# Context sums inside the latent mixer, 96 gathered tokens in both expert layers, and routing in tiles of 128 tokens

## The chip, the core and the metric

The kernel runs on one NeuronCore of a Trainium2 chip. The metric is the device time of one execution in microseconds. Five queues of instructions matter here: PE (TensorE, matrix multiplies; the load of the stationary operand is shown apart as PEld), DVE (VectorE), ACT (ScalarE), POOL (GpSimd, which also issues the gathers of table rows) and SP (which issues the loads of weights). Each runs its instructions in the order in which they were written into it. Everything is in fp32. One matrix multiply of the program is two instructions on PE in the trace, so that counts of the trace are twice those of the program.

## The reference, cut to what matters

The program is a transformer of two layers (`first_block`) whose output is the latent sequence of a second model (`second_block`): 256 latent tokens and 256 context tokens of width 1024. What the change touches lies in the second model:

- a mixer with a recurrent state in layer 0 (`deltanet_mixer`), first over the context, then over the latent tokens, which starts from the state that the context left,
- an attention in layer 1, for which the context gives keys and values,
- after each of them a layer of experts (`peer`), for the context only in layer 0:

```python
qry = (xb @ w_query).reshape(P, PEER_HEADS, 2, PEER_HALF)
s = jnp.einsum('phcd,hckd->phck', qry, sub_keys)
top_s, top_i = lax.top_k(s, PEER_TOPK)          # 16 of 128 keys, two halves, 8 heads
...                                             # the best 16 of the 16 x 16 pairs of each head
act = jax.nn.gelu(jnp.einsum('pd,phkd->phk', xb, u_tab[idx]))
coef = gate * act
return jnp.einsum('phk,phkd->pd', coef, v_tab[idx])
```

So each token has 128 experts out of 16384, with one row of 1024 numbers (4 KB) in `u_tab` and one in `v_tab` for each. A gather of 128 rows is 512 KB.

## The kernel before, in words

**Stages.** In order of time: the context's mixer; the routing of the context's experts (`peer_prep`); the first model, with the context's expert gathers beside it; the latent mixer (`deltanet(E, x, ..., "dl")`); the latent expert layer 0 (`lat_peer(E, 0, ...)`) with the keys of the context for the attention (`ctx_keys`) inside it; the attention; the latent expert layer 1; a last norm.

**Experts of the context.** The dot products with `u_tab` (`gather_dot`) run for all 256 tokens beside the first model. Of the weighted sums over `v_tab`, those of tokens 0 to 127 run there too, on PE (`gather_sum_pe`): for four tokens at a time four gathers bring 128 rows each, eight matrix multiplies of 32 x 512 form the sums (two halves of 512 columns; the four tokens write to different 32 partitions of one PSUM bank), two ACT copies bring them out and one DMA stores four rows. The sums of tokens 128 to 255 run in the latent expert layer 0, on DVE (`bg` and `gather_sum`: 128 gathers, and for each one DVE instruction that adds 128 weighted rows).

**Experts of the latent tokens.** Each layer splits its 256 tokens. The first `NB` of them (64 in layer 0, 96 in layer 1) are gathered: 16 gathers of `u_tab` rows and 16 of `v_tab` rows for each 16 tokens, with one DVE instruction for each (`Few`). The other 192 or 160 tokens go through all 16384 experts densely (`Dense`): 128 tiles of 128 experts, of which each takes 8 multiplies with a tile of `u_tab` (`up`, PE lines `au<-hp,ut`), a gelu and a product with the token's gates in the matrix `G`, and later 8 multiplies with `v_tab` in two halves (`down`, `y<-G,vt`). The gates enter `G` by `spread`: for four tokens a time ACT and DVE make one-hot factors (`ohl`, `ohr`) and PE multiplies them (`gp<-ohr,ohl`). Every tile of `u_tab` or `v_tab` is a load of 512 KB. In time a layer is: routing multiplies (`acs<-hp,w`), the ups with the spreads among them, the first half of the downs, the second half.

**Routing** (`peer_route`). The query multiplies run over all 256 tokens at once (16 tiles of weights, 128 x 256 each); the sorting of the scores (DVE) for the first 128 tokens runs between them, that for the second 128 after them, while the ups go on (`weave`). When a tile of tokens is routed, PE transposes its indices and gates (L1843). The indices of the gathered tokens go through DRAM into another layout (`route`: `gtb`, `ixb`, `fix`).

**What sets the order.** A scheduler puts the instructions of each engine in order from the order in which the program writes them and from its own estimate of times. The side work is written by generators: `start` sets one and its rate, and `tick(E, us)`, called after each tile of the main work, writes `us * rate` steps of it. With `paced` set, such a step is put behind the instruction `E.pin`. In layer 0 the gathers start after the second tile is routed (a factor `z` that is made from the last index and is zero holds them), in layer 1 at up 24 (`FAT`). Gathered rows and weight tiles of a layer share one ring of buffers (`E.wp`, tag `w`, 10 of 512 KB; 8 in the latent mixer, for weights alone).

## Time and profile before

| what | value |
|---|---|
| median of 3 runs (lowest, highest) | 3986.34 us (3985.33, 3995.86) |
| the profiled execution | 3984.59 us, of which its span is 3982.8 us |
| granted clock of PE, mean over the span | 0.951 |
| PE busy | 3528.3 us (89%), 22501 instructions |
| PEld busy | 2828.7 us (71%) |
| DVE, POOL, ACT busy | 2318.4 us (58%), 1247.7 us (31%), 1129.6 us (28%) |
| moved by DMA | 1028.78 MB, mean 258 GB/s |

How to read it: the share of the span that an engine is busy is a mean over stages that differ. Matrix multiplies overlap, so that a group's busy time divided by its count is what one costs in a row, while the "mean ns" of a row is the length of one with its overlap. The granted clock is the share of full speed at which PE was let run. The column "DMA share" is the busy share of the 16 DMA engines; a share of 1 goes with 370 to 400 GB/s here.

The stages by their first and last instructions, for orientation: latent mixer 1668 to 2168 us, latent expert layer 0 2184 to 3099 us, attention until 3225 us, latent expert layer 1 3229 to 3972 us.

### The profile page before, as it was taken

How to read it: one execution, taken by the hardware profiler on the slowest of the kernel's cores; microseconds unless marked ns; L12 is line 12 of the kernel's file. 1: busy time of each engine (PE TensorE's matmuls, PEld its weight loads, DVE VectorE, ACT ScalarE, POOL GpSimd, SP SyncE). 2: the span in 40 equal slices, each digit the busy share in tenths (PEclk: the TensorE clock that was granted, in tenths of full speed). 3: DMA queues.
4: the chain of work that ended last, by engine and by line, in shares of the span. 5: the costliest groups of instructions: out<-in, count | busy, mean ns of one | idle time of the engine just before them, and what ended most of it. 6: DMA issues, size and time to landing. Idle time of an engine off the chain costs nothing. (4 is left out here: it accounts for less than half of the span.)

```text
span 3982.8 us, 60769 instructions
## 1 busy us (share of the span) xinstructions
PE 3528.3 (89%) x22501; PEld 2828.7 (71%) x22501; DVE 2318.4 (58%) x5519; ACT 1129.6 (28%) x3199; POOL 1247.7 (31%) x1169
## 2 busy tenths in 40 slices
PE   7787988979999889888888979988899999998998
PEld 6664564638746458466545979987899668998898
DVE  4774348758646578377732667974530438684442
ACT  4233212634315444242222124720000312470000
POOL 1110004553344553211000255544521104333331
PEclk9898998989999889999999999999999999999999
DMA  5444353899998899633633569999995435999996
GB/s 196 120 141 149 127 179 118 288 332 347 337 343 313 293 328 349 218 118 109 239 115 116 165 260 387 353 392 369 399 340 171 159 95 192 386 356 391 396 392 255
DMA packets 373527, 1028.78 MB, mean 258 GB/s; under 512 B 84240, under 2 KB 86608, under 8 KB 372464
## 3 DMA queue, kind: packets, MB, share of 16 engines
q1 hardware_dynamic: 227728, 557.36, 39.6%
q0 software_dynamic: 119808, 436.26, 29.5%
q10 hardware_dynamic: 25696, 31.28, 2.6%
q8 instruction: 178, 2.92, 0.3%
q14 instruction: 117, 0.96, 0.1%
HBM read 1008.88 MB, written 15.89 MB: 257 GB/s over the span
## 5 line engine op out<-in xcount | busy, mean ns | idle before, releaser
L392 PE MATMUL y<-G,vt 128*128 128x192 f32 (+1 forms) x4096 | 641.2, 316 | 58.4 <-DMA vt<-in_peer_v_dram 58.0
L392 PE MATMUL au<-hp,ut 128*128 128x192 f32 (+1 forms) x4096 | 651.6, 317 | 29.9 <-DMA ut<-in_peer_ut_dram 25.7
L392 PEld LDWEIGHTS y<-G,vt 128*128 128x128 f32 x4096 | 615.0, 191 | 82.8 <-DMA vt<-in_peer_v_dram 64.5
L392 PEld LDWEIGHTS au<-hp,ut 128*128 128x128 f32 x4096 | 624.5, 193 | 40.5 <-issue 29.0
L392 PE MATMUL acc<-hdn,w 128*128 128x256 f32 x1536 | 371.4, 395 | 41.6 <-DVE cvu L1253 16.1
L1697 POOL DMA_INDIRECT gu<-in_peer_u_dram,ixs x256 | 278.8, 1089 | 344.7 <-DVE gu L1699 242.7
L1699 DVE SCALAR_TENSOR_TENSOR gu<-gu,h 128x1024 f32<-128x1024 f32 x256 | 312.0, 1225 | 103.4 <-DMA gu<-in_peer_u_dram,ixs 101.4
L392 PEld LDWEIGHTS acc<-hdn,w 128*128 128x128 f32 x1536 | 292.2, 196 | 96.5 <-issue 23.1
L1718 DVE SCALAR_TENSOR_TENSOR fy<-gv,fc,fy 128x1024 f32<-128x1024 f32 x150 | 192.8, 1285 | 201.6 <-DMA gv<-in_peer_v_dram,fix 201.3
L1789 DVE SCALAR_TENSOR_TENSOR fg<-fg,fh 128x1024 f32<-128x1024 f32 x160 | 193.2, 1227 | 134.6 <-DMA fh<-hl_d 52.6
L1775 POOL DMA_INDIRECT fg<-in_peer_u_dram,fix x160 | 186.7, 1167 | 252.2 <-PE au L392 76.1
L1713 POOL DMA_INDIRECT gv<-in_peer_v_dram,fix x160 | 182.9, 1143 | 244.7 <-PE y L392 204.1
L1713 POOL DMA_INDIRECT gv<-in_peer_v_dram,ixz x128 | 160.1, 1250 | 139.5 <-DVE y L1718 78.8
L1718 DVE SCALAR_TENSOR_TENSOR y<-gv,col,y 128x1024 f32<-128x1024 f32 x127 | 162.8, 1282 | 50.1 <-DMA gv<-in_peer_v_dram,ixz 49.2
L1736 POOL DMA_INDIRECT gv<-in_peer_v_dram,ixT x128 | 140.9, 1101 | 143.2 <-DVE gu L1699 88.2
L392 PE MATMUL acs<-hff,w 128*128 128x256 f32 x704 | 168.7, 380 | 0.0
L392 PE MATMUL acs<-xs,sh 128*128 128x256 f32 x704 | 150.5, 310 | 1.3 <-POOL xs L530 0.8
L392 PEld LDWEIGHTS acs<-hff,w 128*128 128x128 f32 x704 | 126.5, 190 | 21.0 <-issue 7.5
L1456 POOL TENSOR_TENSOR ob<-ob,qs 128x256 f32<-128x256 f32 x32 | 25.0, 781 | 368.2 <-ACT qs L1454 269.0
L1253 DVE SCALAR_TENSOR_TENSOR cvu<-acc,vec,cvu 128x255 f32<-128x255 f32 (+1 forms) x256 | 121.7, 480 | 31.2 <-ACT cvu L1250 29.0
L1943 ACT ACTIVATE ys<-y,ada 128x192 f32<-128x192 f32 (+1 forms) x16 | 5.3, 409 | 455.3 <-PE y L392 455.3
L392 PE MATMUL acs<-hp,w 128*128 128x256 f32 x512 | 117.8, 386 | 8.4 <-DMA w<-in_peer_wq_dram 7.5
(603 smaller groups left out, 6150.4 us busy)
## 6 DMA issues: line engine op xcount, KB each, us to landing
ut<-in_peer_ut_dram SPq DMA_DIRECT2D x256, 512.0 KB
vt<-in_peer_v_dram SPq DMA_DIRECT2D x256, 512.0 KB
w<-in_ada_w_dram SPq DMA_DIRECT2D x96, 512.0 KB
w<-in_dn_w_in_dram SPq DMA_DIRECT2D x96, 512.0 KB
w<-in_w_up_dram SPq DMA_DIRECT2D x88, 512.0 KB
w<-in_peer_wq_dram SPq DMA_DIRECT2D x48, 512.0 KB
wd<-in_w_down_dram SPq DMA_DIRECT2D x44, 512.0 KB
w<-in_w_in_dram SPq DMA_DIRECT2D x40, 512.0 KB
```

The source lines that it names most:

```text
L392: return E.nc.tensor.matmul(out, lhsT=lhsT, rhs=rhs, start=start, stop=stop)
L1253: nc.vector.scalar_tensor_tensor(out=u[:, os], in0=p[:, is_], scalar=cw[tap][:, ct:ct + 1], in1=u[:, os], op0=ALU.mult, op1=ALU.add)
L1456: nc.gpsimd.tensor_tensor(out=ov, in0=ov, in1=qs, op=ALU.add)
L1697: nc.gpsimd.indirect_dma_start(out=g, out_offset=None, in_=E.a["peer_u"], in_offset=bass.IndirectOffsetOnAxis(ap=ix[:, s, k:k + 1], axis=0))
L1699: nc.vector.scalar_tensor_tensor(out=g, in0=g, scalar=1.0, in1=h, op0=ALU.mult, op1=ALU.mult, accum_out=c[:, k:k + 1])
L1713: nc.gpsimd.indirect_dma_start(out=g, out_offset=None, in_=E.a["peer_v"], in_offset=bass.IndirectOffsetOnAxis(ap=ix[:, k:k + 1], axis=0))
L1718: nc.vector.scalar_tensor_tensor(out=y, in0=g, scalar=c[:, k:k + 1], in1=y, op0=ALU.mult, op1=ALU.add)
L1736: nc.gpsimd.indirect_dma_start(out=g, out_offset=None, in_=E.a["peer_v"], in_offset=bass.IndirectOffsetOnAxis(ap=ix, axis=0))
L1775: self.E.nc.gpsimd.indirect_dma_start(out=g, out_offset=None, in_=self.E.a[tab], in_offset=bass.IndirectOffsetOnAxis(ap=self.ix[:, s, k:k ...
L1789: nc.vector.scalar_tensor_tensor(out=g, in0=g, scalar=1.0, in1=h, op0=ALU.mult, op1=ALU.mult, accum_out=self.c[:, s, k:k + 1])
L1943: nc.scalar.mul(s[:, k, nb:256], self.y[k][:, 0:T], g2[:, n * 4 + k:n * 4 + k + 1])
```

## The change

Five edits:

1. The sums of context tokens 128 to 255 leave layer 0 and its DVE code `bg`. They run beside the latent mixer, by `gather_sum_pe`, as 8 groups of 16 tokens. A step of them (one gather; after each fourth also the multiplies, the copies and the store) is written by the mixer's ticks at a rate of `LRATE` = 0.42 per microsecond of its estimated work. The gathered rows take buffers of the mixer's weight ring (`E.wp`), which has 7 instead of 8; the sums take PSUM banks of the tag `ps`, of which the mixer has 2. For this the second tile's indices are transposed as well (`ixT[1]`).
2. Layer 0 gathers 96 tokens instead of 64, as layer 1 does; its dense part has 160 instead of 192. The rate of the gather steps is 0.165 in both, and the second half of the downs is cut at tile 56 instead of 48 (`LAST`).
3. Routing of the latent layers runs one tile of 128 tokens at a time: the query multiplies are 128 x 128, and every tile of query weights is loaded and multiplied twice. In `peer_route` the code for `lin1` does this.
4. The gathers of a layer start as soon as the first tile is routed (`routed`), without the factor `z`. The transposes of the routed indices for both tiles are written 60 steps later (`LAG`), behind an up's last multiply.
5. In `spread` all four `ohl` get the gate on ACT (four instructions of 128 columns instead of two of 128 and one of 256), and DVE makes `ohr` in one instruction of 512 columns instead of one of 256 and two of 128.

```diff
@@ peer_route
+    for ts in ((0, 1),) if lin1 is None else ((0,), (1,)):
+        n = 128 * len(ts)
+        for cidx in range(4):
+            q = PI.tile([128, 4, n], F32, name="pq", bufs=2)
+            ...
+                lin1(ts[0], *z)
+            for j, tt in enumerate(ts):
...
+            if ts[0] == 0:
+                drain(top(0, range(cidx * 4, cidx * 4 + 4)))
@@ gather_sum_pe
-    p = bank(E, "gy", "gy")
+    tag = "gy" if "gy" in E.xps else "ps"
+    p = bank(E, tag, "gy")
-            g = R.tile([128, D], F32, name="gv", tag="g")
-            ix = ixT[:, s * 16 + t + j:s * 16 + t + j + 1]
+            g = (R or E.wp).tile([128, D], F32, name="gv", tag="g" if R else "w")
+            ix = ixT[s // 8][:, s % 8 * 16 + t + j:s % 8 * 16 + t + j + 1]
@@ Dense.prep
-            lin = lambda *z: lin_cols_split(E, PU, None, *z, tag="y", xf=self.x)
+            def lin(tt, ap, off, nt, fn):
+                for t in range(nt):
+                    p = bank(E, "y", "acs")[:, 0:128]
+                    ws = wtile(E, ap, off + t * D * 128, 2, 512)
+                    for k in range(8):
+                        mm(E, p, ws[k // 4][:, k % 4 * 128:k % 4 * 128 + 128], self.x[:, k, tt * 128:tt * 128 + 128],
+                           k == 0, k == 7)
+                    fn(t, p)
...
             def done(t, idx, gate, idf):
                 if t == 0:
                     self.few.route(idx, gate)
+                    routed()
+                found.append((idf[0], idf[1], gate))
+            yield from peer_route(E, P, P, WK, self.i, None, done, lin)
+            for _ in range(LAG):
+                yield
+            for t in range(2):
                 p = pst(E)
+                with tc.issue_after(self.pe):
+                    for j, src in enumerate(found[t]):
+                        nc.tensor.transpose(p[:, j * 128:j * 128 + 128], fl(src), E.ident)
@@ Dense.spread
-        a = 2
-        for j in range(a):
+        for j in range(4):
             nc.scalar.activation(L[:, j], L[:, j], AF.Relu, scale=col(3, j), bias=col(2, j))
-        nc.scalar.activation(L[:, a:4], L[:, a:4], AF.Relu, bias=1.0, scale=-1.0)
-        ...
-        for j in range(a, 4):
-            nc.vector.tensor_scalar(R[:, j], self.iota, col(0, j), col(2, j), op0=ALU.is_equal, op1=ALU.mult)
+        E.pin = nc.vector.tensor_tensor(out=R, in0=self.iota[:, None, :].to_broadcast([128, 4, 128]),
+                                        in1=self.sl[:, 0, t:t + 4, None].to_broadcast([128, 4, 128]),
+                                        op=ALU.is_equal).ins
@@ lat_peer
-                weave(M.prep(P, PU, nm), ups, *WP)
-            z = PW.tile([128, 1], F32, name="z")
-            ...
+                weave(M.prep(P, PU, nm, lambda: start(E, few.steps(), FRATE, 1)), ups, *WP)
@@ constants
-NB, FRATE, FAT, LAST = (64, 96), (0.25, 0.165), 24, 48
+NB, FRATE, LAST, LAG, LRATE = (96, 96), 0.165, 56, 60, 0.42
@@ build
-        with phase(E, "pl", 8, **DNB), tc.tile_pool(name="stl", bufs=1) as PS:
+        with phase(E, "pl", 7, **DNB), tc.tile_pool(name="stl", bufs=1) as PS:
-            deltanet(E, x, A, B, gate, St_d, False, "dl")
+            with tc.tile_pool(name="late", bufs=1, side="right") as R:
+                start(E, chain(*(lambda s=s: gather_sum_pe(E, R, None, s, ixT, co_d, yc_d) for s in range(8, 16))),
+                      LRATE, 0)
+                deltanet(E, x, A, B, gate, St_d, False, "dl")
+                drain(E.beside)
+                E.beside = None
-    def bg(R, z):
-        ...
```

Where instructions move, at three places. The first is PE in the latent mixer, where the 384 multiplies of layer 1's modulation (`acc<-w,cs`, weights `ada_w`) stand beside the steps of the first recurrent scan (`kq`, `tx`, `su`). Before:

```order
L392 MATMUL acc<-w,cs 32x128 x15
L392 MATMUL tx<-X,Rc 64x128 x4
L392 MATMUL acc<-w,cs 32x128 x7
L1097 MATMUL ps<-cst_58,adr 128x128
L392 MATMUL acc<-w,cs 32x128 x25
L392 MATMUL tx<-vn,qkT 64x128 x4
L392 MATMUL su<-vd,krow 128x256 x2
L392 MATMUL kq<-St,kq 64x256 x4
```

And now (`gy<-gv,cT` are the sums of four context tokens):

```order
L392 MATMUL kq<-St,kq 64x256 x4
L392 MATMUL tx<-vn,qkT 64x128 x4
L392 MATMUL acc<-w,cs 32x128 x8
L392 MATMUL tx<-X,Rc 64x128 x4
L392 MATMUL acc<-w,cs 32x128 x16
L392 MATMUL tx<-vn,qkT 64x128 x4
L392 MATMUL acc<-w,cs 32x128 x8
L392 MATMUL gy<-gv,cT 32x512 x8
L392 MATMUL acc<-w,cs 32x128 x8
L1097 MATMUL ps<-cst_58,adr 128x128
L392 MATMUL acc<-w,cs 32x128 x24
L1097 MATMUL ps<-cst_58,adr 128x128
```

The scan ends after the first 24 of the 384 multiplies of the modulation now; before, ten of its sixteen steps ended among them.

The second is SP at the start of the latent mixer, where it issues the weights of the projections (`dn_w_in`). Before:

```order
L328 DMA w<-in_dn_w_in_dram 128x1024 x7
L1424 DMA St<-St_d 128x2x1024
L328 DMA w<-in_dn_w_in_dram 128x1024 x14
L1354 DMA dN<-N 32x8x32 x4
L328 DMA w<-in_dn_w_in_dram 128x1024
```

And now:

```order
L1424 DMA St<-St_d 128x2x1024
L328 DMA w<-in_dn_w_in_dram 128x1024 x2
L1734 DMA cr<-co_d 16x128
L328 DMA w<-in_dn_w_in_dram 128x1024 x2
L1759 DMA yc_d<-gv 4x1024
L328 DMA w<-in_dn_w_in_dram 128x1024 x2
L1759 DMA yc_d<-gv 4x1024
L328 DMA w<-in_dn_w_in_dram 128x1024 x2
L1354 DMA dN<-N 32x8x32 x4
```

After every two weight loads stands the store of a group's sums, which waits for the group's copies.

The third is SP at the start of expert layer 1: query weights, tiles of `u_tab` (`ut`), and the way of the gathered tokens' gates and indices through DRAM. Before:

```order
L328 DMA w<-in_peer_wq_dram 128x1024 x6
L1858 DMA ut<-in_peer_ut_dram 128x1024 x18
L1770 DMA gtb<-gate_23792 96x128
L1858 DMA ut<-in_peer_ut_dram 128x1024
L1771 DMA fg<-gtb 128x6x16
L1858 DMA ut<-in_peer_ut_dram 128x1024 x6
L1770 DMA ixb<-idx_23788 96x128
```

And now:

```order
L328 DMA w<-in_peer_wq_dram 128x1024 x21
L1881 DMA ut<-in_peer_ut_dram 128x1024 x3
L1778 DMA gtb<-gate_24522 96x128
L1881 DMA ut<-in_peer_ut_dram 128x1024
L1779 DMA fg<-gtb 128x6x16
L1881 DMA ut<-in_peer_ut_dram 128x1024 x4
L1778 DMA ixb<-idx_24518 96x128
```

The query weights are loaded twice, and the indices leave behind 8 tiles of `u_tab` instead of 25.

## Rows read from the trace of the kernel before

**Rows 1.** Windows: busy time of each engine by stretch; columns in the first line.
```profile
core 0: us, PE busy (x) PEld busy (x) DVE busy (x) ACT busy (x) POOL busy (x), PEclk, DMA share, GB/s
1668.00:2168.00 500.00, 412.68 (x3645) 287.12 (x3643) 281.10 (x713) 145.58 (x485) 58.18 (x55) 0.94 0.41 137
...
1850.00:1928.00 78.00, 67.40 (x829) 49.60 (x827) 60.67 (x181) 24.18 (x66) 11.88 (x10) 0.93 0.32 92
1928.00:2002.00 74.00, 55.06 (x952) 35.88 (x953) 42.85 (x101) 22.80 (x95) 10.46 (x12) 0.88 0.90 324
...
2184.00:3099.00 915.00, 831.18 (x4962) 792.03 (x4962) 525.14 (x1103) 194.55 (x623) 370.19 (x323) 0.98 0.84 312
3229.00:3972.00 743.00, 697.33 (x4862) 674.77 (x4862) 422.63 (x1014) 162.08 (x531) 252.55 (x243) 0.98 0.88 327
3378.00:3567.00 189.00, 182.82 (x1366) 179.61 (x1365) 138.48 (x346) 119.76 (x417) 70.75 (x63) 0.99 1.01 377
```

**Rows 2.** Groups of expert layer 0: busy, mean ns, idle before and releasers.
```profile
L392 PE MATMUL au<-hp,ut 128*128 128x192 f32 x2048 | 350.3, 330 | 17.2 <-DMA ut<-in_peer_ut_dram 15.5 <-ACT G L1864 1.3 <-ACT cf L1867 0.4
L392 PE MATMUL y<-G,vt 128*128 128x192 f32 x2048 | 349.9, 329 | 37.0 <-DMA vt<-in_peer_v_dram 36.6
...
L392 PE MATMUL kv<-w,hc 128*128 128x512 f32 x32 | 15.1, 593 | 0.0
```

**Rows 3.** Groups of expert layer 1.
```profile
L392 PE MATMUL au<-hp,ut 128*128 128x160 f32 x2048 | 301.3, 305 | 12.8 <-DMA ut<-in_peer_ut_dram 10.3 <-ACT G L1864 0.4
L392 PE MATMUL y<-G,vt 128*128 128x160 f32 x2048 | 291.3, 302 | 21.5 <-DMA vt<-in_peer_v_dram 21.3
...
L392 PE MATMUL acs<-hp,w 128*128 128x256 f32 x256 | 57.5, 379 | 0.9 <-DVE hrow L400 0.9
...
L392 PE MATMUL gp<-ohr,ohl 128*128 128x128 f32 x320 | 42.9, 276 | 0.7 <-ACT G L1902 0.7
```

**Rows 4.** Waits of PE in expert layer 0: total us, times, longest.
```profile
PE y L392 <- DMA vt<-in_peer_v_dram: 36.6, 42, 2.9
PE ps L1843 <- DVE idf L1638: 17.4, 4, 9.0
```

**Rows 5.** Waits of PE in expert layer 1.
```profile
PE y L392 <- DMA vt<-in_peer_v_dram: 21.3, 24, 1.4
PE au L392 <- DMA ut<-in_peer_ut_dram: 10.3, 14, 2.3
PE ps L1843 <- DVE idf L1638: 7.1, 3, 3.6
PE ps L1843 <- DVE z L1988: 2.6, 1, 2.6
```

**Rows 6.** Start of expert layer 1, SP's queue in order of time.
```profile
3315.25 0.33 SPq L1770 DMA_DIRECT2D gtb<-gate  x1
...
3335.89 0.38 SPq L1771 DMA_DIRECT2D fix<-ixb  x1
```

**Rows 7.** Instructions on the gathered tokens' indices, layer 1: duration min/median/max, first and last start.
```profile
L1775 POOL DMA_INDIRECT fg<-in_peer_u_dram,fix x96: 932/938/1987, 3366.9 to 3639.2; - x96
L1713 POOL DMA_INDIRECT gv<-in_peer_v_dram,fix x96: 932/937/1898, 3641.5 to 3918.2; - x96
```

**Rows 8.** Groups of ACT while layer 1 spreads gates, 3378 to 3567 us.
```profile
L1884 ACT ACTIVATE ohl<-ohl,sl 128x128 f32<-128x128 f32 x76 | 34.8, 483 | 0.0
L1885 ACT ACTIVATE ohl<-ohl 128x256 f32<-128x256 f32 x38 | 15.5, 408 | 0.0
```

**Rows 9.** Groups of the whole span: the context sums on PE, tokens 0 to 127.
```profile
L392 PE MATMUL gy<-gv,cT 128*32 128x512 f32 x512 | 73.2, 645 | 18.3 <-DMA gv<-in_peer_v_dram,ixT 12.1 <-ACT gv L1750 6.2
...
L1750 ACT COPY gv<-gy 128x512 f32<-128x512 f32 x64 | 37.4, 584 | 140.9 <-PE gy L392 138.8 <-DMA gu<-in_peer_u_dram,ixs 2.1
```

**Rows 10.** DMA issues: median us from issue to landing, the same gathers.
```profile
gv<-in_peer_v_dram,ixT POOLq DMA_INDIRECT x128, 7.6
```

**Rows 11.** Groups of the latent mixer, 1668 to 2168 us: layer 1's modulation.
```profile
L392 PE MATMUL acc<-w,cs 128*32 128x128 f32 x768 | 31.1, 297 | 2.2 <-DMA w<-in_ada_w_dram 1.8 <-DVE cvu L1253 0.2
```

More of the change, by code (lines that the diff above doesn't have):

```diff
@@ L240, in tick @@
             E.due -= 1
-            if E.paced:
+            if E.paced and E.pin is not None:
                 with E.tc.issue_after(E.pin):
@@ L282, in setup @@
     E.cst, E.xps = {}, {}
-    E.beside, E.due, E.rate, E.last, E.paced, E.first = None, 0, 0, None, 0, None
+    E.beside, E.due, E.rate, E.last, E.paced, E.first, E.pin = None, 0, 0, None, 0, None, None
     load_const(E, E.cp, "cst0")
@@ L1983, in lat_peer @@
                 ups = M.up_first(PU)
-                weave(M.prep(P, PU, nm), ups, *WP)
-            z = PW.tile([128, 1], F32, name="z")
-            def wait(col):
-                E.pin = nc.vector.tensor_scalar(z, col, 0.0, 0.0, op0=ALU.is_ge, op1=ALU.mult).ins
-            other = None
-            if beside is not None:
-                wait(M.sl[:, 0, 255:256])
-                other = beside(PB, z)
-                start(E, chain(lambda: other, lambda: few.steps(z)), FRATE[i], 1)
-            else:
-                M.at[FAT] = lambda col: (wait(col), start(E, few.steps(z), FRATE[i], 1))
+                weave(M.prep(P, PU, nm, lambda: start(E, few.steps(), FRATE, 1)), ups, *WP)
             with tc.tile_pool(name=nm + "H", bufs=1) as PH:
@@ L2233, in build @@
         store(xc_d, xc)
-    ixT = PB.tile([128, 128], I32, name="ixT")
+    IXc = tc.tile_pool(name="ixt", bufs=1)
+    IX = IXc.__enter__()
+    ixT = [IX.tile([128, 128], I32, name=f"ixT{t}") for t in range(2)]
     A, B = ada_gain(E, m0, 3, 1, vec("n20"), "a2c")
```

70 lines of the change are left out of this document (25 added, 45 removed).

## The prediction

> **What bounds the kernel now.** I read the windows first, one for each stage that the change touches, then for both expert layers the groups of PE and the waits of PE, and at last what the trace has of the gathers. The windows [rows 1] are to be read by two columns, PE busy and DMA share. In expert layer 0 PE is busy for 831.2 of 915 us at a DMA share of 0.84, in layer 1 for 697.3 of 743 us at 0.88; between 3378 and 3567 us, the stretch of the spreads, both are full (182.8 of 189 us, share 1.01). So an expert layer is PE's work, and what PE waits for is mostly a tile of a table that DMA brings late, and the indices of the routing [rows 4, 5]. The latent mixer is another thing: PE is busy for 412.7 of 500 us while DMA is at 0.41 [rows 1]. It has room for transfers and little for multiplies. The change moves 128 gathers with their sums from a stage where DMA is full to one where it isn't, and pays on PE there.
>
> **Expert layer 0.** Here the trace holds the answer almost as it stands: layer 1 already has the split of 96 gathered and 160 dense tokens, the same tables' sizes and no context sums beside it. Layer 0 after the change is layer 1 before it, plus the keys of the context. Layer 1 takes 743 us [rows 1]. The keys add 15.1 us of multiplies [rows 2]; what DVE, ACT and POOL do for them lies beside the downs. That makes 758 instead of 915 us: -157 us. The parts agree with it: the ups and downs cost 350.3 + 349.9 us at 192 columns and 301.3 + 291.3 us at 160 [rows 2, 3], which is 107.6 us of PE, and the rest is waits for tiles and indices that go down with the bytes. From below the gain is these 107.6 us alone, if layer 0 kept every wait of its own; from above it is 172 us, if the keys cost nothing. I take 157, since it is a measured whole and the two layers' code is the same.
>
> **Routing one tile at a time.** The query multiplies were 256 instructions of 256 columns for 57.5 us in a layer [rows 3]; they become 512 of 128 columns. The nearest row of that shape is the spread's `gp` with 42.9 us for 320, 134 ns each [rows 3]: 512 x 0.134 = 68.6 us, 11 us more, and 22 us for both layers. The bounds are 57.5 us again (no gain in 128 columns lost, 0) and the 147 ns that one of 160 columns costs (301.3 / 2048, [rows 3]), 18 us more a layer. I take the row of the same shape. The second load of the query weights falls into a stretch before the gathers, and costs nothing unless DMA is full there; the 8 MB at the rate of the spreads (377 GB/s, [rows 1]) would be 22 us a layer.
>
> The Trainium skill has a figure for this too: TensorE: Matmul & The Clock Gate, section Back-to-back issue gap, says that in a stream of loads and multiplies one of 128 columns comes every 81 ns. By it the 512 would take 41 us, 16 us less than now, and the sum below would be 55 us lower. The row of 128 columns in this trace has 134 ns, so I give that figure no chance of its own.
>
> **What comes earlier by it.** Before, the indices of the gathered tokens were back from DRAM at 3335.9 us, 107 us after the layer's start [rows 6], and the first gather went at 3366.9 us [rows 7], since it was held to up 24. Now the first tile's multiplies take half of 68.6 us, and the sorting follows without those of the second: 107 - 57.5 + 34 = about 84 us after the start, so the gathers begin some 50 us earlier in layer 1 and end some 50 us earlier than their 3918.2 us [rows 7]. The pressure on DMA in the downs is less for that long. PE waited 21.3 + 10.3 us for tiles in layer 1 [rows 5]; I take 5 us of it off in each layer, -10 us (bounds 0 and -63). The transposes of the indices stand 60 steps later, so that PE's waits for them, 7.1 + 2.6 us [rows 5], go: -19 us for both layers (layer 0 now counted as layer 1; bounds 0 and -19). What is late next there is the gathered rows: they share the ring of ten buffers with the tiles, so a late `fix` would hold tiles. SP sends `gtb` behind three tiles now; the gate was there at 3315.3 us, 86 us after the start [rows 6], and by the same reckoning it comes at some 63 us, before PE is through with the query weights at 69. So SP isn't held.
>
> **Spread.** ACT gets four instructions of 0.458 us (34.8 / 76) instead of two of them and one of 0.408 (15.5 / 38) [rows 8]: 0.51 us more for each of 40 spreads, 20 us in a layer. ACT is busy for 119.8 of these 189 us and would be for 140, under PE's 182.8 [rows 1], so I count 0. If that cover fails it is 20 us a layer.
>
> **The latent mixer.** On PE come 32 groups of four tokens. The same number of groups beside the first model cost 73.2 us of PE and 18.3 us of waits for gathered rows and copies [rows 9]. Of the 73.2 us some fall into gaps: PE is idle for 87.3 us, of which 19 lie in the stretch of the modulation, 1928 to 2002 us [rows 1], where now hardly a group stands. Of the other 68 us I let half be filled, -34. The third place is the order itself. The modulation's weights bind DMA (share 0.90, 324 GB/s), so this stretch keeps its length; PE did 55.1 us of work in it, of which only 31.1 are the modulation [rows 1, 11]. The other 24 us are steps of the scan, which now stand ahead of it, with nothing to hide behind: +24. POOL issues 128 gathers and is otherwise busy for 58 us; ACT's 64 copies are 37.4 us [rows 9] in an engine busy for 145.6 of 500 [rows 1]: nothing beyond the waits counted. The sum is 73 + 18 - 34 + 24 = +81 us. From below it is 0 (all of the groups in idle time, the scan as before), from above 73 + 18 + 24 = 115.
>
> **Sum.** -157 + 22 - 10 - 19 + 0 + 81 = -83 us. The profiled execution took 3984.6 us, 1.7 us less than the median shown, so 3901.6 us for it and 3903 us for the median. What the trace can't give is how the first model's order shifts a little with the second `ixT`; I count nothing for it.
>
> **The rivals.**
>
> *The ring of seven buffers makes the mixer wait (slower).* A group holds four of the seven buffers until its last gather has landed and its sums are copied, and SP, which waits in order, has a store of sums after every two weight loads. Then each of the 32 groups stops the stream of weights. It speaks for it that a gather takes 7.6 us to land [rows 10], longer than one tile of weights lasts PE; against it that beside the first model, with DMA nearly full, a group waited for only 18.3 / 32 = 0.6 us [rows 9], though with buffers of its own. Without the mixer the change is worth -164 us; groups and order cost up to 97; so it decides from a stop of 67 / 32 = 2.1 us a group on. With half of the landing time, 3.8 us, the mixer costs 97 + 122 = 219 and the kernel is at 3986 + 55 = 4041 us.
>
> The Trainium skill gives the landing a smaller price: DMA: Bandwidth & Descriptors, section Anatomy of one DMA, puts a gather of 512 KB at 2.0 us + bytes / 436e3, which I work out to an estimate of 3.2 us. Half of that is under the 2.1 us, and this rival would not come out slower. The trace's 7.6 us are with DMA almost full, which the mixer is not, so the truth may lie between.
>
> *The mixer takes the sums for little.* If the gaps take nearly all of the groups and the scan goes on filling the modulation, the mixer costs the 18 us of waits and some 10 us of groups that find no gap, 28 instead of 81: 3850 us. The DMA share of 0.41 and the 87 us of idle PE speak for it; the chain of the scan, whose gaps are single microseconds, and the new order of PE against it.
>
> *The spread is bound by ACT.* With 20 us in each layer, 3943 us. ACT's 140 of 189 us speak against it, the alternation of ACT, DVE and PE within a spread for it.
>
> *Layer 0 gains only its columns.* -107.6 instead of -157, with the mixer at its bound of 115: -107.6 + 22 - 10 - 19 + 115 = 0, so 3987 us. Against it stands that layer 1 runs without those waits.
>
> **How the numbers follow.** Chances: the forecast 0.64; the cheap mixer 0.12; ACT 0.12; layer 0's columns alone 0.04; the ring 0.08. Two measurements of this kernel can be told apart from 0.3% on, 12 us. The first three end under 3974 us: faster 0.88; the fourth is no change, 0.04; the ring is slower, 0.08. The forecast's own range takes the mixer from 45 to 115 us and layer 0 from 135 to 172: 3880 to 3955 us. For 8 in 10 it has to reach the cheap mixer: 3850 to 3955 us.
>
> **What would show it.** Right: expert layer 0 at about 750 us, ups and downs at 128 x 160 with some 300 us each; the query multiplies near 69 us; the first gather of layer 1 about 85 us after the layer's start; no wait of PE for `idf`; the mixer at about 580 us with 70 to 75 us of `gy`, and PE idle for longer while `ada_w` loads. Wrong: waits of SP or PE for sums and gathered rows in the mixer of more than 67 us in sum, ACT as the releaser of PE in the spreads, or tiles of `u_tab` that come late in the first 44 ups because gathered rows hold the ring.

## The result and the profile after: 0.5 % slower

The changed kernel takes 4018.3 us (median of 12 runs, 3999.1 to 4023.4), the kernel before 3993.6 us (12 runs beside them, 3985.3 to 4005.9): ratio 1.0053, 95 % interval 1.0039 to 1.0067. The forecast was 3903 us with a range up to 3955. The profiled execution has a span of 4018.0 us, against 3982.8 before.

The windows of the changed kernel, one for each stage that the prediction priced (columns as in [rows 1]: length, busy time of each engine with its instructions, granted TensorE clock, DMA share, GB/s): latent mixer, expert layer 0, expert layer 1.
```profile
core 0: us, PE busy (x) PEld busy (x) DVE busy (x) ACT busy (x) POOL busy (x), PEclk, DMA share, GB/s
1676.00:2346.00 670.00, 515.43 (x4171) 313.98 (x4167) 288.08 (x713) 183.84 (x558) 185.15 (x183) 0.89 0.60 203
2363.00:3139.00 776.00, 722.22 (x5186) 698.15 (x5185) 421.17 (x955) 184.73 (x598) 268.61 (x259) 0.98 0.90 336
3268.00:4009.00 741.00, 699.31 (x5118) 682.77 (x5118) 414.22 (x941) 174.90 (x577) 251.81 (x243) 0.99 0.92 339
...
```
Against [rows 1], layer 0 went from 915 to 776 us (-139), layer 1 from 743 to 741, and the mixer from 500 to 670 (+170). The mixer starts 8 us later. The sum is +37 us; the spans differ by 35. So the layers paid nearly what was forecast, and the mixer took more than that back.

The groups of PE in the changed layer 0 (busy, mean ns, idle before and its releasers), which answer to [rows 2], with the query multiplies:
```profile
L392 PE MATMUL au<-hp,ut 128*128 128x160 f32 x2048 | 302.2, 305 | 20.2 <-DMA ut<-in_peer_ut_dram 18.0
L392 PE MATMUL y<-G,vt 128*128 128x160 f32 x2048 | 293.6, 304 | 22.4 <-DMA vt<-in_peer_v_dram 22.3
L392 PE MATMUL acs<-hp,w 128*128 128x128 f32 x512 | 63.6, 283 | 7.8 <-DMA w<-in_peer_wq_dram 7.8
...
L392 PE MATMUL kv<-w,hc 128*128 128x512 f32 x32 | 15.1, 593 | 0.0
...
```
Ups and downs are 104 us shorter, as [rows 3] had promised. The waits for `idf` of [rows 4, 5] are in no list any more. The first `fg` goes out 83 us after the layer's start, and 82 us after it in layer 1, for which 84 was forecast. The query multiplies take 63.6 us here and 60.9 in layer 1, under the 68.6 of the forecast: 0.12 us each.

Now the mixer, cut by its own landmarks: from the last start of the gates' multiplies `acc<-w,hdn` to the first of layer 1's modulation, the modulation, and from there to the last add to `x`. First the kernel before, then the changed one:
```profile
1692.00:1925.00 233.00, 198.41 (x1570) 158.91 (x1570) 169.15 (x440) 78.05 (x245) 32.24 (x24) 0.95 0.37 112
1925.00:2001.00 76.00, 56.70 (x1015) 36.87 (x1007) 45.73 (x107) 24.41 (x101) 10.46 (x12) 0.89 0.90 320
2001.00:2168.00 167.00, 144.84 (x993) 83.17 (x993) 56.60 (x152) 36.31 (x129) 10.52 (x15) 0.97 0.24 82
sum 476.00, PE 399.95 PEld 278.96 DVE 271.48 ACT 138.77 POOL 53.22; mean PE 133.32 PEld 92.99 DVE 90.49 ACT 46.26 POOL 17.74
```
```profile
1705.00:2083.00 378.00, 287.12 (x2106) 190.62 (x2104) 218.67 (x527) 116.96 (x350) 120.09 (x113) 0.89 0.59 188
2083.00:2159.00 76.00, 48.64 (x813) 27.29 (x814) 3.85 (x21) 11.03 (x44) 10.65 (x12) 0.76 0.90 348
2159.00:2346.00 187.00, 165.99 (x1163) 87.16 (x1161) 55.52 (x150) 48.16 (x152) 46.59 (x53) 0.96 0.54 185
sum 641.00, PE 501.75 PEld 305.06 DVE 278.04 ACT 176.15 POOL 177.34; mean PE 167.25 PEld 101.69 DVE 92.68 ACT 58.72 POOL 59.11
```
Of 165 us, 145 lie ahead of the modulation, where the weights of the projections stream, none in the modulation, 20 behind it. PE is busy for 101.8 us more and idle for 63.2 us more. The groups of PE in the same stretch say what it did, first the projections' multiplies before (the 476 us), then the changed kernel (the 641 us):
```profile
L392 PE MATMUL acc<-hdn,w 128*128 128x256 f32 x754 | 178.3, 389 | 19.9 <-DVE cvu L1253 9.0 <-issue 7.3 <-ACT t L1167 1.4
```
```profile
L392 PE MATMUL acc<-hdn,w 128*128 128x256 f32 x754 | 191.6, 411 | 39.5 <-DMA w<-in_dn_w_in_dram 34.8 <-issue 1.7 <-ACT t L1167 1.4
L392 PE MATMUL gy<-gv,cT 128*32 128x512 f32 x512 | 71.8, 657 | 26.2 <-DMA gv<-in_peer_v_dram,ixT 20.7 <-DVE N L1311 1.5 <-issue 1.2
...
L392 PE MATMUL acc<-w,cs 128*32 128x128 f32 x768 | 40.1, 343 | 19.8 <-DMA w<-in_ada_w_dram 19.8
...
```
The sums' multiplies take 71.8 us, as priced by [rows 9]. Nearly all of the other 30 us are the old multiplies, which became dearer at the same counts: the projections' took 178.3 us and take 191.6, the modulation took 31.1 us in [rows 11] and takes 40.1, and the granted clock of the mixer between its landmarks fell from 0.95 to 0.90 of full speed. The waits are for tiles of weights (34.8 and 19.8 us) and for gathered rows (20.7), 75 us together; before, the first and the last kind weren't there.

How one such wait goes on, in the changed kernel's PE queue (start, length, idle before):
```profile
2086.61 0.65 PE L392 MATMUL acc<-w,cs 128*32 128x128 f32 x16
2093.96 3.64 PE L392 MATMUL gy<-gv,cT 128*32 128x512 f32 x16 [6.71 <-DMA gv<-in_peer_v_dram,ixT]
2097.38 1.08 PE L392 MATMUL acc<-w,cs 128*32 128x128 f32 x16
```
PE stands still for 6.71 us, behind a group whose last row hasn't landed, with other multiplies queued behind it. The next sixteen multiplies of the modulation take 1.08 us, where sixteen took 0.65 just before: the granted clock was 1.00 between 2086.0 and 2087.3 us and is 0.50 from 2093.96 to 2098.5 us, after the standstill. These are its two levels, 2.4 and 1.2 GHz.

And SP in the mixer (what its queue waited for: us in total, times, longest):
```profile
SPq L328 <- PE gy L392: 107.4, 18, 17.5
SPq L328 <- PE acc L392: 103.2, 51, 13.2
SPq L1759 <- ACT gv L1758: 85.4, 20, 16.6
SPq L328 <- DMA yc_d<-gv: 39.7, 14, 4.9
...
```
L328 issues the weights. They wait for buffers that gathered rows hold (107.4 and 39.7 us), and behind stores of sums that aren't copied yet (85.4). This is the rival of the ring of seven, or looks like it; the experiments test it.

### The profile page after: what moved, and what is told of

The parts are those of the page before. It is cut to its first block, busy times and chain, and to the rows that moved or that the text cites. A ratio compares the mean times of both kernels' runs of the same rounds, so it can differ in the third digit from the quotient of the medians.

```text
span 4018.0 us, 62899 instructions
## 1 busy us (share of the span) xinstructions
PE 3536.9 (88%) x23502; PEld 2775.0 (69%) x23502; DVE 2215.5 (55%) x5300; ACT 1167.1 (29%) x3290; POOL 1273.0 (32%) x1233
## 3 DMA queue, kind: packets, MB, share of 16 engines
q1 hardware_dynamic: 233312, 575.32, 40.3%
## 5 line engine op out<-in xcount | busy, mean ns | idle before, releaser
L392 PE MATMUL au<-hp,ut 128*128 128x160 f32 x4096 | 603.2, 304 | 38.1 <-DMA ut<-in_peer_ut_dram 33.3
L392 PE MATMUL y<-G,vt 128*128 128x160 f32 x4096 | 585.1, 304 | 38.6 <-DMA vt<-in_peer_v_dram 37.8
L392 PEld LDWEIGHTS au<-hp,ut 128*128 128x128 f32 x4096 | 572.5, 193 | 53.4 <-issue 41.6
L392 PEld LDWEIGHTS y<-G,vt 128*128 128x128 f32 x4096 | 568.4, 193 | 55.7 <-DMA vt<-in_peer_v_dram 39.1
L392 PE MATMUL acc<-hdn,w 128*128 128x256 f32 x1536 | 388.3, 409 | 60.1 <-DMA w<-in_dn_w_in_dram 34.8
L1744 POOL DMA_INDIRECT gv<-in_peer_v_dram,ixT x256 | 269.2, 1052 | 509.2 <-PE gy L392 137.0
L392 PE MATMUL gy<-gv,cT 128*32 128x512 f32 x1024 | 150.3, 673 | 41.0 <-DMA gv<-in_peer_v_dram,ixT 33.2
L1253 DVE SCALAR_TENSOR_TENSOR cvu<-acc,vec,cvu 128x254 f32<-128x254 f32 (+1 forms) x256 | 121.9, 478 | 76.0 <-ACT cvu L1250 73.3
L1904 ACT ACTIVATE ohl<-ohl,sl 128x128 f32<-128x128 f32 x320 | 138.8, 531 | 0.0
L1758 ACT COPY gv<-gy 128x512 f32<-128x512 f32 x128 | 74.7, 585 | 215.4 <-PE gy L392 184.9
L392 PE MATMUL acs<-hp,w 128*128 128x128 f32 x1024 | 124.4, 279 | 8.7 <-DMA w<-in_peer_wq_dram 7.8
```

The costliest lines, as they stand in the source:

```text
L392: return E.nc.tensor.matmul(out, lhsT=lhsT, rhs=rhs, start=start, stop=stop)
L1253: nc.vector.scalar_tensor_tensor(out=u[:, os], in0=p[:, is_], scalar=cw[tap][:, ct:ct + 1], in1=u[:, os], op0=ALU.mult, op1=ALU.add)
L1744: nc.gpsimd.indirect_dma_start(out=g, out_offset=None, in_=E.a["peer_v"], in_offset=bass.IndirectOffsetOnAxis(ap=ix, axis=0))
L1758: nc.scalar.copy(gs[0][:, n * 512:n * 512 + 512], p)
L1904: nc.scalar.activation(L[:, j], L[:, j], AF.Relu, scale=col(3, j), bias=col(2, j))
```

## The experiments

All have the changed kernel as their base. "Above e1" is the difference of the ratios times 3991 us; with the intervals of the run and of e1 together it is known to 14 to 21 us either way.

| run | median us | ratio to before, 95 % | above e1 |
|---|---|---|---|
| changed kernel | 4018.3 | 1.0053 (1.0039, 1.0067) | 176 |
| e1 no sums | 3842.6 | 0.9613 (0.9580, 0.9646) | 0 |
| e2 multiplies only | 3899.6 | 0.9763 (0.9733, 0.9792) | 60 |
| e3 gathers only | 3881.0 | 0.9718 (0.9684, 0.9751) | 42 |
| e9 both, unlinked | 3965.3 | 0.9945 (0.9927, 0.9962) | 132 |
| e4 four buffers apart | 4034.8 | 1.0106 (1.0073, 1.0138) | 197 |
| e5 stores by ACT | 4027.2 | 1.0089 (1.0057, 1.0122) | 190 |
| e6 a tile for the sums | 3998.4 | 1.0014 (1.0000, 1.0029) | 160 |
| e7 e5 and e6 | 4014.5 | 1.0053 (1.0034, 1.0072) | 176 |
| e8 e1, one transpose | 3835.7 | 0.9613 (0.9592, 0.9633) | 0 |
| e10 e6, burst | 4002.9 | 1.0023 (1.0006, 1.0039) | 164 |
| e11 ring of eight | 4000.7 | 1.0022 (1.0004, 1.0041) | 163 |
| e12 burst, ring of eight | 3989.5 | 0.9999 (0.9983, 1.0016) | 154 |
| e13 half the groups | 3919.5 | 0.9822 (0.9792, 0.9851) | 83 |
| e14 half here, half in layer 0 | 4002.2 | 1.0034 (1.0014, 1.0055) | 168 |
| e15 all in layer 0 | 4018.1 | 1.0077 (1.0048, 1.0106) | 185 |
| e16 half rows, 8 buffers | 4039.1 | 1.0118 (1.0076, 1.0160) | 201 |
| e17 half rows, 6 buffers | 4065.0 | 1.0183 (1.0141, 1.0224) | 227 |
| e18 sums on DVE | 3985.1 | 0.9999 (0.9982, 1.0015) | 154 |

### What the mixer's term is made of

**e1.**
```diff
-start(E, chain(*(lambda s=s: gather_sum_pe(E, R, None, s, ixT, co_d, yc_d) for s in range(8, 16))), LRATE, 0)
+nc.sync.dma_start(yc_d[128:256], x[1])
```


> The changed kernel without the sums of context tokens 128 to 255 in the latent mixer (those rows of the context's sums are filled with one store of other data); all else as changed. Theory A (the whole loss is in the mixer, the expert layers gain what they gained): the mixer goes back from 670 to about 500 us and the kernel to 4019 - 170 = 3850 us. Theory B (the tables' layers or the first model lost something through the new order): the mixer still takes well over 500 us or the kernel stays over 3880 us.

Theory A: between its landmarks the mixer is back at 477 us (476 before). Everything else together is worth 154 us (141 to 168), where the prediction had 164 without the mixer.

**e2** (`xm` is `x[0]`; `R` is given for the first model's sums alone). In e2 and e9 the sums are copied to a tile of their own, as in e6 below.
```diff
-            gs.append(g)
+            if R:
...
+            else:
+                gs.append(xm)
```


> The mixer's 32 groups keep their multiplies, copies and stores but read rows that lie in SBUF already, so no row is gathered and no buffer of the weights' ring is taken (the sums are of wrong rows). Theory A1 (the ring of seven: weights wait behind gathered rows): the mixer costs what the multiplies cost beside its gaps, 40 to 75 us over e1, about 3890 to 3925 us. Theory A2 (the groups' multiplies and copies in the chain of the scan cost more than their time): nearly the whole 170 us stay, 4000 us or more.

**e3.**
```diff
+def rows_only():
+    for k in range(128):
+        g = E.wp.tile([128, D], F32, name="gv", tag="w")
+        nc.gpsimd.indirect_dma_start(out=g, out_offset=None, in_=a["peer_v"],
+                                     in_offset=bass.IndirectOffsetOnAxis(ap=ixT[1][:, k:k + 1], axis=0))
+        yield
```


> The mixer's 128 gathers go into the ring of seven as in the changed kernel, but nothing reads the rows: no multiplies, no copies, no stores (the sums are left out). Theory A1 (a group holds four buffers until its multiplies, copies and store are through): a buffer is free again once its row has landed, so little is left, 10 to 40 us over e1, 3860 to 3890 us. Theory A3 (the 67 MB of transfers themselves delay the mixer's weights and round trips): 60 us or more over e1, 3910 us or more.

**e9.**
```diff
-            gs.append(g)
+            gs.append(g if R else xm)
```


> Every gather, multiply, copy and store of the mixer's sums at its place, and the ring of seven as it is, but the multiplies read rows that lie in SBUF, not the gathered ones (the sums are of wrong rows; nothing reads the gathered ones). Theory D1 (the loss comes from rows that keep ring buffers until their multiplies have their turn on PE): what multiplies and gathers cost by themselves adds up, 3843 + 57 + 38 = 3938 us, give or take 12. Theory D2 (PE, DMA and POOL are simply full together, whoever holds a buffer): 3985 us or more.

The mixer between its landmarks in e1, e2, e3 and e9, one row each:
```profile
1703.00:2180.00 477.00, 403.51 (x3572) 281.89 (x3566) 273.75 (x698) 139.22 (x474) 54.10 (x51) 0.94 0.41 135
```
```profile
1698.00:2226.00 528.00, 470.07 (x4076) 292.53 (x4072) 275.19 (x698) 177.06 (x548) 54.53 (x51) 0.96 0.38 123
```
```profile
1705.00:2212.00 507.00, 406.64 (x3568) 283.06 (x3562) 275.85 (x697) 138.23 (x474) 169.79 (x171) 0.93 0.76 254
```
```profile
1705.00:2300.00 595.00, 488.04 (x4083) 300.70 (x4078) 276.04 (x697) 174.06 (x546) 171.97 (x171) 0.90 0.67 218
```
Multiplies alone bring 66.6 us of PE, of which 15.6 go into its idle time (73.5 to 57.9 us): a quarter. The granted clock is 0.96, against 0.94 in e1. Gathers alone, which nobody reads, bring 27 us of idle PE. The medians of both, 3900 and 3881 us, lie where theory A1 had them. Both, unlinked, bring 84.5 us of PE, 18 more than the multiplies by themselves, and 33.5 us of idle time: 132 us by the ratios, 30 more than 60 + 42 (23 either way, by the intervals of the four runs). The windows show 118 us of it; e1's profiled execution was 6 us above its median. Neither D1's 3938 nor D2's 3985 came; it stands between. The linked kernel costs 43 us more than e9 (9 either way).

What delays PE in e3 isn't late weights: PE waits 6.5 us for them there and 6.0 in e1. DVE and ACT wait for POOL for 49 us instead of 14, and for the solve's transfers through DRAM for 45 us instead of 33. In e3 POOL stands still before its gathers for 219 us, 139 of them for earlier rows that are still on their way into the ring. Steps of the scan that POOL has to do stand behind in its queue. One of them (DVE's and POOL's lines in order of time: start, length, idle before):
```profile
1856.58 0.17 DVE L407 TENSOR_SCALAR cvr<-cvr 128x8 f32<-128x8 f32 x1 [1.18 <-ACT cvq L1276]
1865.40 0.94 POOL L2286 DMA_INDIRECT gv<-in_peer_v_dram,ixT  x1 [7.92 <-DMA Tc<-dT]
1866.37 1.67 POOL L409 TENSOR_TENSOR l2r<-cvr,mhalf 128x8 f32<-128x8 f32 x1
1868.07 1.29 DVE L1284 TENSOR_TENSOR krow<-st,l2r 128x512 f32<-128x512 f32 x2 [11.32 <-POOL l2r L409]
```
`l2r` reads `cvr`, which is there at 1856.8 us; it starts 9.6 us later, behind a gather before which POOL stood still for 7.92 us. So the 42 us are the price of the gathers with their place in POOL's queue and in the ring. How much of it the transfers themselves cost is not shown: no run has them without the gathers on POOL.

Between e9 and the changed kernel the order differs too, and no expectation counted that. The scheduler puts 15 of the 16 steps of the first scan ahead of the modulation in the changed kernel, and 7 in e9 (PE's groups ahead of the modulation, eight instructions a step, the changed kernel first):
```profile
L392 PE MATMUL tx<-vn,qkT 64*64 64x128 f32 x120 | 11.2, 312 | 13.4 <-DVE vd L1468 13.3 <-ACT vn L1465 0.2
```
```profile
L392 PE MATMUL tx<-vn,qkT 64*64 64x128 f32 x56 | 4.6, 282 | 0.0
```
So the 43 us hold two things, which no run takes apart: the link (multiplies that wait for their rows, buffers that wait for the multiplies, the copies and the stores) and the scan's steps that have lost the modulation to stand beside.

### What the link's price hangs on

**e4.**
```diff
-with phase(E, "pl", 7, **DNB), tc.tile_pool(name="stl", bufs=1) as PS:
+with phase(E, "pl", 4, **DNB), tc.tile_pool(name="stl", bufs=1) as PS:
...
+        tc.tile_pool(name="lateg", bufs=4, side="right") as RG:
```


> The sums as changed, but the gathered rows have four buffers of their own and the weights four (instead of seven for both). Theory A1: the 35 us that PE waits for weights of the projections and most of the 20 us for the modulation's go, and with them part of the low clock: 3940 to 3980 us. Theories A2 and A3: no ring, no help: 4010 us or more, as only four buffers are left for weights.

No gain. The waits of PE in e4's mixer:
```profile
PE gy L392 <- DMA gv<-in_peer_v_dram,ixT: 80.6, 14, 20.7
PE acc L392 <- DMA w<-in_ada_w_dram: 21.4, 26, 3.8
...
```
The waits for the projections' weights are gone, as theory A1 said, those for the modulation's have stayed, and 60 us more of waits for rows have come in: POOL can't fetch the next group before the one ahead is summed and stored (its gathers wait 263 us for multiplies of the sums and 32 us for stores).

**e5.**
```diff
-nc.sync.dma_start(y_d[s * 16 + t:s * 16 + t + 4], gs[0][0:128:32])
+(nc.sync if R else nc.scalar).dma_start(y_d[s * 16 + t:s * 16 + t + 4], gs[0][0:128:32])
```


> The sums as changed, but their stores go out on ACT's queue instead of SP's. Theory B1 (SP, which waits in order, holds the weights behind a store whose sums aren't copied yet; its waits for the copies were 85 us): the loss over what multiplies alone and gathers alone cost (3843 + 57 + 38 = 3938 us against 4018) goes for the most part, 3950 to 3980 us. Theory B2 (the four buffers of a group are held until the copy and the store are through, whoever issues the store): 4005 us or more. Theory B3 (what PE waits for is the landing of a group's last row): 4005 us or more.

**e6.**
```diff
-nc.scalar.copy(gs[0][:, n * 512:n * 512 + 512], p)
+nc.scalar.copy(yp[:, n * 512:n * 512 + 512], p)
...
-nc.sync.dma_start(y_d[s * 16 + t:s * 16 + t + 4], gs[0][0:128:32])
+nc.sync.dma_start(y_d[s * 16 + t:s * 16 + t + 4], yp[0:128:32])
```


> The sums are copied to a tile of their own and stored from there, still by SP, so that the four gathered rows give their buffers back as soon as the multiplies are through, and not after the copies and the landing of the store. Theory B2: the 80 us of loss go for the most part, 3950 to 3980 us. Theory B1: SP still stands behind each copy, 4005 us or more. Theory B3: 4005 us or more.

**e7**, with the edits of e5 and e6.

> e5 and e6 together. Theories B1 and B2, whichever holds: 3940 to 3970 us. Theory B3 (the rows' landing before the multiplies is what PE and the ring wait for): still 3995 us or more.

B1 falls: SP's 85 us behind the copies cost nothing that e5 gives back. B2 holds for 16 us at most, a fifth of what it claimed. e7, with both edits, gives nothing. B3 had e5 and e7 right and e6 within 7 us, but none of the three tests it by itself.

**e10.**
```diff
-            if j < 3:
+            if j < 3 and R:
                 yield
...
-        yield
+        for _ in range(1 if R else 4):
+            yield
```


> As e6 (sums in a tile of their own), and the four gathers of a group are issued together, right before its multiplies, with four steps of the beside work behind them, instead of one gather at a step. The first row of a group then is not held for three more steps. Theory D1: less time in the ring, 3950 to 3980 us against 3998 of e6. Theory D2, or a hold that is the landing and PE's turn and not the spacing of the gathers: 3990 us or more; four transfers at once may also hold the weights longer, 4010 us.

**e11**, and **e12** with the burst of e10.
```diff
-with phase(E, "pl", 7, **DNB), tc.tile_pool(name="stl", bufs=1) as PS:
+with phase(E, "pl", 8, **DNB), tc.tile_pool(name="stl", bufs=1) as PS:
```


> The changed kernel with a ring of eight buffers in the mixer instead of seven (the index tile's pool keeps one buffer less). Theory D1: one more buffer lets one more weight tile go ahead of a group, 3990 to 4005 us against 4018. Theory D2: no difference, 4018 us.

> The four gathers of a group together, as in e10, on the ring of eight, the sums stored from a gathered row's buffer as in the changed kernel. Theory D1: both gains add up, 3955 to 3990 us. Theory D2: 4010 us or more.

The burst on top of e6 gives nothing, an eighth buffer some 12 us (its interval still touches the changed kernel's), burst and eighth buffer 22. e12 is level with the kernel before. The order goes along: of the first scan's steps 1 stands beside the modulation in the changed kernel and in e5, 2 in e7, 3 in e6, 4 in e10 and e11, 6 in e12 and 9 in e9. So what e6, e11 and e12 give back can be the order as well as the buffers.

**e16**, with eight half rows apart and four weights' buffers, and **e17**, with six and five.
```diff
-g = (R or E.wp).tile([128, D], F32, name="gv", tag="g" if R else "w")
+g = R.tile([128, 512], F32, name="gv", tag="g")
```


> The sums as changed, but each gather brings half a row (512 columns, 256 gathers of 256 KB instead of 128 of 512 KB) into eight half-size buffers apart from the weights, which have four: room for two groups of four. If the link's price is the waits (weights behind rows in the changed kernel, 35 us; rows in e4, 81 us), both go: 3965 us (as e9, unlinked) to 3980 us, faster than before. If POOL's 128 further gathers of 0.94 us, or transfers of half the size, cost as much as that, 4000 us or more.

> As e16 with six half-size buffers and five for the weights: room for one group and a half. If the next group's rows must be on their way while one is summed, it stands between e4 and e16, 3980 to 4015 us; if weights had been short with four buffers, it is below e16.

e16 came out as the second half of its expectation had it, at 4000 us or more; e17's expectation missed. PE's waits in e16's mixer:
```profile
PE gy L392 <- DMA gv<-in_peer_v_dram,ixT: 31.6, 15, 3.7
...
PE acc L392 <- DMA w<-in_ada_w_dram: 21.6, 25, 3.0
PE tx L392 <- DVE vd L1468: 21.4, 6, 7.4
...
```
With room for two groups the waits for rows fell from 80.6 to 31.6 us, and the kernel didn't get faster than e4; e17, with room for one and a half, is slower. e16 also doubles the gathers, so it doesn't price a second group's room by itself. Rows in a place of their own were tried in three sizes and helped in none.

**e18.**
```diff
-start(E, chain(*(lambda s=s: gather_sum_pe(E, R, None, s, ixT, co_d, yc_d) for s in range(8, 16))),
-      LRATE, 0)
+start(E, gather_sum(E, ixT[1], c, y), LRATE, 0)
```


> The 128 gathers of the mixer at their rate into the ring of seven, with tokens on the partitions, each row added on DVE when it lands (128 operations of 1.28 us, 164 us, as beside layer 0 before); no multiplies, no groups, one store at the end. Theory G1 (the price is PE's standing still for a group of four, and the groups' hold of buffers): DVE has 203 idle us of 477 in e1; 3843 + 38 of the gathers + a third to a half of 164 = 3935 to 3965 us, faster than both kernels. Theory G2 (the scan's chain passes through DVE as it passes through PE, and every operation put into it is paid in full): 3843 + 38 + 164 = 4045 us.

In between: 154 us above e1. If the gathers' 42 are taken off, 112 of DVE's 164 are left; that the two add up is not shown. Level with the kernel before, like e12, and with nothing of the sums on PE; so the price doesn't hang on PE alone. PE's waits there:
```profile
PE zt L392 <- DMA Tc<-dT: 37.9, 1, 37.9
PE tx L392 <- DVE vd L1468: 26.0, 12, 9.0
...
PE acc L392 <- DVE cvu L1253: 25.4, 9, 8.3
...
```
These are the scan's own links through DVE (and the solve, which DVE works out and `Tc` brings back through DRAM); the first of them, 37.9 us, is not among PE's waits in e1.

### The other side of the term, and the density

**e13.**
```diff
-start(E, chain(*(lambda s=s: gather_sum_pe(E, R, None, s, ixT, co_d, yc_d) for s in range(8, 16))),
-      LRATE, 0)
+start(E, chain(*(lambda s=s: gather_sum_pe(E, R, None, s, ixT, co_d, yc_d) for s in range(8, 12))),
+      LRATE / 2, 0)
```


> Only context tokens 128 to 191 are summed in the mixer, spread over its whole length at half the rate; the sums of 192 to 255 are left out (their rows are filled by one store of other data). Theory F1 (each group has its price): half of 176 us over e1, 3843 + 88 = 3931 us. Theory F2 (the price comes from groups that crowd the ring of seven): half of what multiplies and gathers cost unlinked, 3843 + 28 + 19 = 3890 us, up to 3905 us.

F1: half the groups cost 83 us (18 either way), nearly half of 176, so some 5 us a group; F2's 47 to 62 us lie outside of that. But half of what e9 cost, 66 us, lies at its edge; that crowding adds nothing is not shown.

**e15** and **e14.**
```diff
+def rest(R):
...
+    yield from gather_sum(E, ix, c, y)
...
-lat_peer(E, 0, *pi, m0[:, 40:48, 0], "p0", rows, hl_d, keys)
+lat_peer(E, 0, *pi, m0[:, 40:48, 0], "p0", rows, hl_d, keys, rest)
```


> The changed expert layers (96 gathered tokens, routing by tile), and all of tokens 128 to 255 summed on DVE beside expert layer 0 as before the change, none in the mixer. The prediction's term for layer 0 rested on the sums' leaving: their 67 MB at 377 GB/s are 178 us, of which some 78 fit into the tenth of 776 us that DMA is idle; so 100 to 150 us over e1, 3943 to 3993 us. If PE's columns had been the bound and the sums hidden: under 3900 us.

> Tokens 128 to 191 are summed in the mixer, at half the rate and with a ring of eight; tokens 192 to 255 beside expert layer 0 on DVE (64 gathers, two halves of the indices on 128 partitions, added at the end). The 33.5 MB cost layer 0 between 45 us (with its DMA at 0.90 some transfers fit) and 89 us (all of them at the 377 GB/s of the spreads). Theory F2: 3890 + 45 to 70 = 3935 to 3960 us, faster than both kernels. Theory F1: 3931 + 45 to 89 = 3975 to 4020 us.

In e15 the sums' gathers stand ahead of the layer's own. Beside layer 0 with its new split the same sums cost 185 us (167 to 203), more than the 100 to 150 that were expected: about the 178 us of their bytes at the rate of the spreads in [rows 1], at a DMA share of 0.94, so that hardly anything of it was hidden. What PE waits for in e15's layer 0:
```profile
PE y L392 <- DMA vt<-in_peer_v_dram: 84.2, 65, 4.4
PE au L392 <- DMA ut<-in_peer_ut_dram: 61.2, 31, 8.2
...
```
In the changed kernel these were 22.3 and 18.0. So the layer's gain hangs on the sums' leaving; with the sums left there the new split and routing would have cost 31 us (e15 against before). The mixer charges as much as the layer did, and the division of e14 pays about the same, as F1 had it (3975 to 4020 us).

**e8.**
```diff
-        xf = WK.tile([128, 128], F32, name="xf", bufs=1)
+        if t == 0:
+            xf = WK.tile([128, 128], F32, name="xf")
```


> e1 (no sums in the mixer) with the indices of the context's second tile not transposed any more, as before the change. The latent mixer's first multiplies came 11 us later in e1 than in the kernel before, and no term of the prediction counted that. Theory C1 (the second transpose moves the order of the first model): these some 10 us go, 3832 us. Theory C2 (the pools' places or the expert routing's code move it, or it is spread from run to run): 3843 us as e1.

The ratio is that of e1 (0.9613), which speaks for C2; with the intervals of the two, the 10 us of C1 are not ruled out. In every run with the new code the mixer's first multiplies come 6 to 26 us later than in the profile of before, whose execution was itself 9 us under the 3993.6 of its runs. What is left of that, if anything, wasn't settled.

## Why the prediction was wrong

**The layers and the routing: right.** -157 + 22 - 10 - 19 = -164 us; e1 has -154 (-168 to -141), and e15 shows that the sums' leaving was what it hung on. What the narrower split gives by itself was not run; with the bytes left there it gave nothing, where the prediction had read 107.6 us of the gain as PE's columns. Layer 0 gained 139 and not 161 us: it takes about 35 us more than layer 1 (776 against 741), not 15.1. Beside the keys' multiplies it has 7 us of PE for their norm, transposes and the gain's row, a wait of 4.7 us for that row, and 40.3 us of waits for tiles where layer 1 has 30.8. The second load of the query weights was hidden: PE waits for them once, for 7.8 us at the start of layer 0, where it waited 7.5 before. ACT didn't hold the spreads (`gp` waited 1.0 and 1.5 us for it). The 5 us a layer for earlier gathers didn't come: PE's waits for tiles in layer 1 are 30.8 us where [rows 5] had 31.6, moved from the downs to the ups:
```profile
PE y L392 <- DMA vt<-in_peer_v_dram: 15.5, 21, 1.3
PE au L392 <- DMA ut<-in_peer_ut_dram: 15.3, 16, 3.6
...
```
The first of these rows answers to the 21.3 of [rows 5], the second to the 10.3.

**The latent mixer: wrong, and by itself the whole error.** The term was 73 + 18 - 34 + 24 = +81 with 115 as the upper bound; it measured 176. Piece by piece:
- 73 of multiplies: 71.8. Right.
- -34, half of PE's idle time filled: e2 filled 15.6. Much of the idle time of this stage is waits for the scan's links through DVE and ACT, often of about one microsecond (e1: 14.1 us for `vd` in 13 waits). A group in PE's order, 2.1 us in e2 (67.8 / 32), fills a gap and delays the link behind it.
- 24 for the scan's steps displaced from the modulation: the displacement came. Of 25 us of such steps beside the modulation 2 are left; the stretch is 76 us in both, now with its own multiplies 9 us dearer and 26.5 us of waits for weights and a row in it. What the displacement cost is not shown apart. In e2 and e9, where nothing waits for a row, the steps stayed there.
- 18 of waits, taken from the first model [rows 9]: PE is idle for 63 us more, and waits 75 us for rows and weights. There the rows had eight buffers apart from the weights; here seven serve both.
- Not in the sum at all: the gathers' own price (42 us in e3, with nobody waiting for a row), and the 30 us by which the old multiplies became dearer at the lower clock. With multiplies alone (e2) they didn't, in sum; with gathers beside (e9) multiplies old and new became 18 us dearer, without a wait for a row.

Without gathers the term was about right, by luck: 73 - 34 + 24 = 63 against e2's 60, with 18 us too much taken off for gaps and 24 us put in for a displacement that e2 doesn't have. What comes with the gathers was put at 18 us and measured 176 - 60 = 116: 42 for the gathers alone, some 30 for gathers and multiplies together, 43 for the link with its order.

The failed step is these 18 us: the waits priced from the first model, and the sentence that found "nothing beyond the waits counted" in POOL and ACT, with a DMA share of 0.41 taken for room. The runs showed 116 us in their place. POOL's low busy share hid that it stands in order before gathers with the scan's steps behind it (e3), and PE stands in its order before groups with the scan's steps behind them. How the 42 us divide into POOL's queue, ring and transfers, and the 43 us into the link and the order, stays open.

**The rival of the ring.** It was given 0.08, with a stop of 2.1 us a group as the point where the change turns slower, and 4041 us. By its own reckoning (176 - 97) / 32 = 2.5 us came, past that point, so its price was near; and SP's waits for sums and gathered rows passed the 67 us that were to be the sign of it. Its mechanism holds in part at most: an eighth buffer and a tile for the sums give 12 and 16 us back, with another order. But rows apart from the weights (e4, e16) only exchange waits for weights against waits for rows. That PE stands still in its order for whichever comes last is what the linked runs share.

The Trainium skill's figure in DMA: Bandwidth & Descriptors, section Anatomy of one DMA, gave an estimate of 3.2 us for a gather's landing, and by it this rival would not have come out slower. In the changed mixer, at a DMA share of 0.61, the median from issue to landing is the last number of this row:
```profile
gv<-in_peer_v_dram,ixT POOLq DMA_INDIRECT x125, 5.7
```
The measurement decides: under load the landing was nearly twice the estimate. The Trainium skill's 81 ns for a multiply of 128 columns, in TensorE: Matmul & The Clock Gate, section Back-to-back issue gap, isn't borne out either: 63.6 / 512 = 124 ns an instruction, in fp32.

**The chances.** 0.88 on faster rested on this one term; its bounds were worked out from the pieces that I had listed, and what I had left out was larger than the term. The range of 3880 to 3955 us doesn't follow from its own bounds either: the mixer at 45 and layer 0 at 172 give 3852 us, 115 and 135 give 3959. The measured time lies outside of both.

## What to carry to other kernels

Price a move at both ends in the same way: the sums' bytes were worth 185 us where they left and cost 176 us where they went, although one stage had DMA at 0.84 and the other at 0.41. A low busy share in a stage that is a chain of small links is not room, and a queue that works in order isn't free while it waits: look at what stands behind each moved instruction. Leave the moved work out there, and put in its multiplies alone, its transfers alone and both unlinked, before the whole is built. When two stages charge the same for each part, as these two did, dividing the work between them gains nothing.

## What the runs showed of the hardware that was not expected

Gathers whose rows nobody reads delayed the kernel by 42 us (23 to 61 by the intervals of e3 and e1), at 254 GB/s, well under the 377 of the spreads, and without making PE wait longer for weights; POOL's queue, in which the scan's steps stood behind them, has a part in it. And in e9 the multiplies became 18 us dearer than in e2 without any wait for a row, at a mean granted clock of 0.90, where e2 had 0.96 with the same multiplies. PE was idle for 107 us there and for 58 in e2; that the gathers lower the clock through this idle time is likely, but not shown apart.
